# 32 more tokens as gathered expert rows, and a gate matrix added up in DRAM by indirect DMAs

## The chip, the cores and the metric

One core of a Trainium2 chip. The metric is the device time of one execution in microseconds; the time before is the median of three runs.

## What is computed

One layer of a decoder for 512 tokens of 2048 float32 features: two token mixers, a merge, a PEER channel mixer, a gated per-layer input and a last norm. The change lies in the PEER mixer. Per token it scores 8 heads against two tables of 128 keys, takes the 16 best of each half, then the 16 best of their 256 sums; each of these 8 x 16 = 128 choices is one of 16384 experts, with a softmax gate g:

```
z = jnp.einsum('thkd,td->thk', u_tab[eb], hb)
a = jax.nn.gelu(z, approximate=False) * gb
return jnp.einsum('thk,thkd->td', a, v_tab[eb])
```

`eb` are a token's 128 expert numbers, `gb` its gates, `u_tab` and `v_tab` tables of 16384 rows of 2048 floats (128 MB each).

## The kernel before, in words

The tokens are in two groups, and each group has its own way through the PEER mixer.

**Group A, the gathered rows** (128 tokens, one to a partition). For each of its 128 choices s an indirect DMA on POOL (`gather`, L777) fetches 128 rows of 2048 floats, one per token, into one of two buffers `row`. In the u loop VectorE multiplies the row with the token's h and sums it up (`dot_u`, L783; the instruction is L785); in the v loop it adds the row, times its coefficient, to `outA` (`axpy_v`, L1078; L1083). Each of these steps sends the gather for the choice two further on, into the buffer that it has just freed.

**Group B, the dense path** (the other 384 tokens). All 16384 experts are computed: the u loop has 128 steps, each with a block of 128 experts: 16 x 3 = 48 matmuls of 384 columns (`mm3`, L146 to L149; three products of parts, hi and lo, for float32 accuracy). ScalarE takes GELU and stores the result in DRAM (`finish`, z_s). The v loop multiplies z by the gate matrix G (`act_mul`), splits the product into two parts (`act_split`) and multiplies it with the v table: again 128 steps of 48 matmuls, whose sums VectorE adds up (`add_up`, L1091).

**The weights** come through `Ahead`: SP loads a block two steps ahead, ScalarE (L111) and VectorE (L112) split it into hi and lo one step ahead, in four buffers each. Without these splits TensorE has nothing to multiply.

**The gate matrix** has a place for every expert and every token of group B, nearly all zeros. `gate_tokens` (L821) builds it in the u loop: for four tokens at a time ScalarE and VectorE make one-hot matrices (L832, L833, L838), TensorE multiplies them (L843), ScalarE and VectorE bring the result into `stage` (L848, L849), and ACT's queue stores 32 tokens at a time in DRAM (G_s). The v loop loads G by `act_load`.

**Order.** In both loops the order on every engine is the order of the program's text (`tc.manual_schedule`, L871). A list `work` spreads the top-k steps of group B's three blocks of 128 tokens and the building of G over the steps of the u loop: 16 steps of top-k alone, twice 36 steps with the top-k of the next block and G of the last one, then 22 steps with G alone. `dots` spreads the dot products evenly, about 1.07 a step.

Of the kernel before, what the change touches and what calls it, by code (L numbers as in the profile page):

```python
# [20 lines left out]
T = 512  # L21
D = 2048
KT = 16
NA = 128
NB = T - NA
NJ = 8
# [20 lines left out]
def kernel(ctx: ExitStack, tc: tile.TileContext, a, dbg=None):  # L47
# [14 lines left out]
    # ---------------------------------------------------------------- helpers  # L62
# [14 lines left out]
    class Ring:  # L77
        """Buffers taken in turn."""
# [42 lines left out]
    class Ahead:  # L121
        """Streams of a list of blocks: loaded two steps ahead, split one step ahead."""
# [28 lines left out]
    def split(hi, lo, src, gain=None):  # L151
        """hi + lo = src * gain, both float32r."""
# [29 lines left out]
    def rstd_cols(ss, n, name):  # L182
        """[128 tokens, blocks] of 1/sqrt(ss/n + eps)."""
# [13 lines left out]
    def sums_over_features(sq):  # L197
        """[128 tokens, 4] PSUM sums over the partitions of sq [128, T]."""
# [6 lines left out]
    def rows_of(rc, out=None):  # L205
        """[128, tokens], in out or else in PSUM: every partition holds the row of rc."""
# [11 lines left out]
    class SumSq:  # L218
        """Sum of squares of [128, T] chunks over features."""
# [18 lines left out]
    # ---------------------------------------------------------------- constants  # L238
    masks = const.tile([128, 384], F32R, name="masks")
    cst = const.tile([128, 386], F32, name="cst")  # L240
    negmask, ident, iota = cst[:, :128], cst[:, 128:256], cst[:, 256:384]
    freq, sgn = cst[:, 384:385], cst[:, 385:386]
    tril = const.tile([128, 128], U32, name="tril")
# [16 lines left out]
    # ---------------------------------------------------------------- DRAM scratch  # L260
# [7 lines left out]
    z_s = dram.tile([128 // NJ, 128, NJ, NB], F32, name="z_s")  # L268
# [31 lines left out]
    # ---------------------------------------------------------------- HGRN2  # L300
# [147 lines left out]
    # ---------------------------------------------------------------- gates (kept before the sigmoid)  # L448
    def gate_proj(src, dst):
        ps = cols_proj(src, xh, xl)  # L450
# [4 lines left out]
    # ---------------------------------------------------------------- MLA  # L455
# [17 lines left out]
    # rotary tables: angle = position * frequency, reduced to [-pi, pi]  # L473
# [49 lines left out]
    for hp in range(4):  # L523
# [21 lines left out]
        # a head's rotary part: its 64 rows of high parts, and in the other 64 rows their low parts  # L545
# [58 lines left out]
    # ---------------------------------------------------------------- merge  # L604
# [33 lines left out]
    opool.release()  # L638

    # ---------------------------------------------------------------- residual, second norm  # L640
# [20 lines left out]
    hBl = hpool.tile([128, 16, NB], F32R, name="hBl")  # L661
    hrow = hpool.tile([128, D], F32, name="hrow")
# [38 lines left out]
    def topk(b, i1o, i2o, gate):  # L701
        """Steps (cost, function) that fill i1o, i2o, gate: [128 tokens, 8 heads * 16] float32."""
# [57 lines left out]
    # ---- group A: expert rows gathered for the first 128 tokens  # L760
    def prep_A():
# [3 lines left out]
        def experts():  # L765
            V.scalar_tensor_tensor(i1, i1, 128.0, i2, op0=OP.mult, op1=OP.add)
            V.tensor_copy(eA, i1)
            gather(a["peer_u"], 0)
            gather(a["peer_u"], 1)
# [5 lines left out]
    in_flight = {}  # L775

    def gather(tab, s):  # L777
        row = rows()
        G.indirect_dma_start(out=row, out_offset=None, in_=tab,  # L779
                             in_offset=bass.IndirectOffsetOnAxis(ap=eA[:, s:s + 1], axis=0))  # L780
        in_flight[s] = row

    def dot_u(s):  # L783
        row = in_flight.pop(s)
        V.scalar_tensor_tensor(row, row, 1.0, hrow, op0=OP.mult, op1=OP.mult,  # L785
                               accum_out=zA[:, s:s + 1])
        if s + 2 < 128:
            gather(a["peer_u"], s + 2)
        else:
            gather(a["peer_v"], s + 2 - 128)  # L790

    # ---- group B: the gate matrix [i1, i2, token]
    slots = {}
    after_pe, after_pe_next, hold = [], [], [0]

    def prep_B(b):
        i1 = upool.tile([128, 128], F32, name="i1", bufs=2)
        i2 = upool.tile([128, 128], F32, name="i2", bufs=2)
        gt = upool.tile([128, 128], F32, name="gt", bufs=1)

        def turn():
            slots[b] = upool.tile([128, 4, 128], F32, name="slots", bufs=1)

            def pe():
                ps = mx()
                for n, t in enumerate((i1, i2, gt)):
                    TE.transpose(ps[:, n * 128:n * 128 + 128], t, ident)

                def act():
                    S.activation(flat(slots[b][:, :2]), ps[:, :256], AF.Copy)  # L810
                    split(slots[b][:, 2].bitcast(F32R), slots[b][:, 3], ps[:, 256:384])
                return act

            after_pe.append(lambda: after_pe_next.append(pe))
            hold[0] = 2

        return topk(b + 1, i1, i2, gt) + [(0, turn)]

    stage = [None]

    def gate_tokens(t0):  # L821
        """Gate matrices of tokens t0 .. t0+3 of group B."""
        if t0 % TC == 0:
            stage[0] = upool.tile([128, 128, TC], F32, name="stage", bufs=1)
        st = stage[0]
        hot = []
        for i in range(4):
            b, t = divmod(t0 + i, 128)
            l = upool.tile([128, 128], F32R, name="ohl", bufs=8)
            r = upool.tile([128, 2, 128], F32R, name="ohr", bufs=8)  # L830
            i1T, i2T = (slots[b][:, n, t:t + 1] for n in range(2))
            S.activation(l, iota, AF.Abs, scale=-1.0, bias=i1T)  # L832
            V.scalar_tensor_tensor(r, iota[:, None, :].to_broadcast([128, 2, 128]), i2T,  # L833
                                   slots[b][:, 2:4, t:t + 1].to_broadcast([128, 2, 128]),
                                   op0=OP.is_equal, op1=OP.mult)
            hot.append((l, r))
        for l, _ in hot:
            S.activation(l, l.bitcast(F32), AF.Relu, scale=-1.0, bias=ones[:, :1])  # L838
# [537 lines left out]
```

## Time and profile before

| | us |
|---|---|
| median of three runs (4041.59 to 4042.62) | 4041.68 |
| span of the profiled execution | 4040.0 |
| u loop, end of its first step to its end | 1651.7 to 2771.2 |
| v loop | 2771.2 to 3838 |
| first and last one-hot matmul | 1853.4 to 2679.3 |

The profiled execution's own time outside the profile is not listed apart from its span; the median of the runs is 1.7 us above the span. Times in the rows below count from the start of the span. A busy share is an average over stages; what an engine waits for in one stage is read in the table of stretches and in the timelines. PE is TensorE, PEld its weight load, DVE VectorE, ACT ScalarE, POOL GpSimd, SP the engine whose queue loads the weights.

### The profile page before, as it was taken

The numbers are of one execution on the slowest core, as the hardware profiler recorded it, in microseconds if no ns is written. First come the engines' busy times: TensorE is split into PE (matmuls) and PEld (weight loads), VectorE is DVE, ScalarE is ACT, GpSimd is POOL, SyncE is SP. The second block draws the span as 40 slices with busy tenths as digits, with TensorE's granted clock in tenths as the row PEclk, the third lists the DMA queues.
The fourth block names the chain that finished last, engine by engine and source line by source line (L and its number), as shares of the span: only waits on it lengthen the run. The fifth ranks groups of instructions, "written<-read, shape, count | busy, mean of one in ns | idle before, by whom it ended". The sixth has DMA issues, their size and how long they took to land. (4 is left out here: it accounts for less than half of the span.)

```text
span 4040.0 us, 54629 instructions
## 1 busy us (share of the span) xinstructions
PE 4005.3 (99%) x21191; PEld 3667.2 (91%) x21191; DVE 2621.1 (65%) x3992; ACT 1597.2 (40%) x2582; POOL 347.6 (9%) x262
## 2 busy tenths in 40 slices
PE   9999999999999999999999999999999999999998
PEld 7878777778888889999999999999999999999976
DVE  5352554443343343699998998977777888877744
ACT  5342433332332242325566555753333333333443
POOL 0000000000000000021221211111111111111000
PEclk9999999999999999999999999999999999999999
DMA  5222222334444442478787788789888888888432
GB/s 210 97 74 94 72 96 84 102 105 141 151 141 133 141 140 99 166 286 304 283 303 283 287 302 298 293 332 356 317 297 315 312 311 312 299 313 310 169 117 97
DMA packets 264515, 862.68 MB, mean 214 GB/s; under 512 B 24128, under 2 KB 94272, under 8 KB 229568
## 3 DMA queue, kind: packets, MB, share of 16 engines
q1 hardware_dynamic: 202064, 531.57, 38.5%
q0 software_dynamic: 36864, 268.45, 17.8%
q10 hardware_dynamic: 25328, 59.17, 3.8%
q8 instruction: 168, 2.75, 0.3%
q14 instruction: 91, 0.75, 0.1%
HBM read 780.44 MB, written 78.64 MB: 213 GB/s over the span
## 5 line engine op out<-in xcount | busy, mean ns | idle before, releaser
L111 ACT ACTIVATE hi<-raw 128x1024 fp32r<-128x1024 f32 x806 | 851.4, 1059 | 1606.9 <-PE acc L148 1371.9
L112 DVE TENSOR_TENSOR lo<-raw,hi 128x1024 fp32r<-128x1024 f32 x806 | 975.0, 1221 | 782.6 <-ACT hi L111 779.5
L147 PE MATMUL acc<-hBh,hi 128*128 128x384 f32 x2304 | 775.0, 336 | 0.0
L148 PE MATMUL acc<-hBl,hi 128*128 128x384 f32 x2304 | 774.5, 336 | 0.0
L149 PE MATMUL acc<-hBh,lo 128*128 128x384 f32 x2304 | 774.4, 336 | 0.0
L148 PEld LDWEIGHTS acc<-hBl,hi 128*128 128x128 f32 x2304 | 433.1, 188 | 3.0 <-DVE hBl L155 0.2
L147 PEld LDWEIGHTS acc<-hBh,hi 128*128 128x128 f32 x2304 | 433.1, 188 | 2.7
L149 PEld LDWEIGHTS acc<-hBh,lo 128*128 128x128 f32 x2304 | 433.1, 188 | 0.0
L779 POOL DMA_INDIRECT row<-in_peer_u_dram,eA x128 | 198.9, 1554 | 2551.1 <-DMA raw<-in_uT_dram 1703.2
L149 PE MATMUL acc<-xh,lo 128*128 128x512 f32 x912 | 363.9, 399 | 0.0
L147 PE MATMUL acc<-xh,hi 128*128 128x512 f32 x912 | 363.4, 398 | 0.0
L148 PE MATMUL acc<-xl,hi 128*128 128x512 f32 x912 | 362.6, 398 | 0.0
L147 PE MATMUL acc<-ahx,hi 128*128 128x384 f32 x1024 | 344.7, 337 | 0.0
L148 PE MATMUL acc<-alx,hi 128*128 128x384 f32 x1024 | 344.1, 336 | 0.0
L149 PE MATMUL acc<-ahx,lo 128*128 128x384 f32 x1024 | 344.1, 336 | 0.0
L147 PE MATMUL acc<-ah,hi 128*128 128x384 f32 x1024 | 344.1, 336 | 0.0
L148 PE MATMUL acc<-al,hi 128*128 128x384 f32 x1024 | 344.1, 336 | 0.0
L149 PE MATMUL acc<-ah,lo 128*128 128x384 f32 x1024 | 344.1, 336 | 0.0
L1083 DVE SCALAR_TENSOR_TENSOR outA<-row,coef,outA 128x2048 f32<-128x2048 f32 x127 | 298.0, 2346 | 16.6 <-DMA row<-in_peer_v_dram,eA 16.3
L785 DVE SCALAR_TENSOR_TENSOR row<-row,hrow 128x2048 f32<-128x2048 f32 x128 | 292.0, 2283 | 20.5 <-DMA row<-in_peer_u_dram,eA 20.4
L779 POOL DMA_INDIRECT row<-in_peer_v_dram,eA x128 | 147.5, 1152 | 860.3 <-DVE outA L1083 799.6
L149 PEld LDWEIGHTS acc<-xh,lo 128*128 128x128 f32 x912 | 171.4, 188 | 43.0 <-issue 2.4
(379 smaller groups left out, 6270.5 us busy)
## 6 DMA issues: line engine op xcount, KB each, us to landing
raw<-in_uT_dram SPq DMA_DIRECT2D x256, 512.0 KB, 6.9
raw<-in_vB_dram SPq DMA_DIRECT2D x256, 512.0 KB, 5.7
z_s<-t ACTq DMA_DIRECT2D x128, 192.0 KB, 4.9
G_s<-stage ACTq DMA_DIRECT2D x12, 2048.0 KB, 14.4
zt<-z_s SPq DMA_DIRECT2D x32, 768.0 KB, 7.4
gt<-G_s SPq DMA_DIRECT2D x32, 768.0 KB, 12.1
raw<-in_w_ga_dram SPq DMA_DIRECT2D x32, 512.0 KB, 3.5
raw<-in_w_gb_dram SPq DMA_DIRECT2D x32, 512.0 KB, 3.5
```

The lines of the kernel that those rows point to most:

```text
L111: S.activation(hi, raw, AF.Copy)
L112: V.tensor_tensor(lo, raw, hi.bitcast(F32), op=OP.subtract)
L147: TE.matmul(out, lhsT=lh, rhs=rh, start=start, stop=False)
L148: TE.matmul(out, lhsT=lh, rhs=rl, start=False, stop=False)
L149: TE.matmul(out, lhsT=ll, rhs=rh, start=False, stop=stop)
L779: G.indirect_dma_start(out=row, out_offset=None, in_=tab, in_offset=bass.IndirectOffsetOnAxis(ap=eA[:, s:s + 1], axis=0))
L785: V.scalar_tensor_tensor(row, row, 1.0, hrow, op0=OP.mult, op1=OP.mult, accum_out=zA[:, s:s + 1])
L1083: V.scalar_tensor_tensor(outA, row, coef[:, s:s + 1], outA, op0=OP.mult, op1=OP.add)
```

## The change

NX = 32 of the 384 tokens of group B move to the gathered rows; the dense path keeps ND = 352. The 32 tokens are the last of group B. They use all 128 partitions: each token has RX = 4 partitions, each with 32 of its 128 choices (`eX`, `gateX`, `zX`, `hrowX`, `outX`), so there are 32 more gathers for u and 32 more for v. `gather`, `dot_u` and `axpy_v` take their choices from one list, `order`; per step of either loop there are 1.33 dots or additions. At the end the four partial sums of a token are added up (`finish_x2`).

The one-hot matrices go. `clear` fills G_s with zeros, four expert blocks with each of the 32 gate projections that precede the PEER mixer. In the u loop `places` computes where in G_s each gate belongs, and `scatter` adds 128 gates (one choice of 128 tokens; 96 tokens in the last block) into G_s with an indirect DMA that accumulates: 3 x 128 scatters, in heads of 16. The scatters of one head do not wait for one another; those of the next head wait for all 16 of the head before, as two heads can choose the same expert. Blocks come in the order 2, 0, 1. POOL's order is no longer that of the text: the compiler's scheduler places its DMAs.

```diff
+NX = 32
+RX = 128 // NX
+ND = NB - NX
-    G_s = dram.tile([NB // TC, 128, 128 * TC], F32, name="G_s")
+    G_s = dram.tile([128, 128, ND], F32, name="G_s")
...
+    def clear(j0):
+        nc.scalar.dma_start(G_s.rearrange("j i t -> i j t")[:, j0:j0 + 4], zeros[:, None, :].to_broadcast([128, 4, ND]))
+
     def gate_proj(src, dst):
+        clear(4 * (32 - len(gates_todo) - 1))
...
+    order = [(a["peer_u"], 0, s) for s in range(128)] + [(a["peer_u"], 1, s) for s in range(NX)]
+    order += [(a["peer_v"], 1, s) for s in range(NX)] + [(a["peer_v"], 0, s) for s in range(128)]
+
+    def gather():
+        if order:
+            tab, x, s = order.pop(0)
+            row = rows()
+            e = eX if x else eA
+            G.indirect_dma_start(out=row, out_offset=None, in_=tab,
+                                 in_offset=bass.IndirectOffsetOnAxis(ap=e[:, s:s + 1], axis=0))
+            in_flight.append((row, x, s))
+
+    def dot_u():
+        row, x, s = in_flight.pop(0)
+        z = zX if x else zA
+        V.scalar_tensor_tensor(row, row, 1.0, hrowX if x else hrow, op0=OP.mult, op1=OP.mult,
+                               accum_out=z[:, s:s + 1])
+        gather()
...
+        def places():
+            off_b[b] = upool.tile([128, 128], U32, name="off", bufs=2)
+            V.scalar_tensor_tensor(i2, i2, 128.0, i1, op0=OP.mult, op1=OP.add)
+            V.tensor_scalar(i2, i2, float(ND), tcol[:, b:b + 1], op0=OP.mult, op1=OP.add)
+            V.tensor_copy(off_b[b], i2)
...
+    def scatter(b, s):
+        n = min(128, ND - 128 * b)
+        ins = G.indirect_dma_start(out=G_flat, in_=gate_b[b][:n, s:s + 1], in_offset=None,
+                                   out_offset=bass.IndirectOffsetOnAxis(ap=off_b[b][:n, s:s + 1], axis=0),
+                                   compute_op=OP.add).ins
+        if s % 16 == 0:
+            before_head[b], this_head[b] = this_head.get(b, []), []
+        for other in this_head[b]:
+            tc.declare_no_dep(ins, other, reason="a head's experts differ")
+        for other in before_head[b]:
+            tc.add_manual_dep(ins, other.name, SYNC, reason="experts of two heads can be the same")
+        this_head[b].append(ins)
+
+    def gate_tokens(b, s0):
+        for s in range(s0, s0 + 4):
+            scatter(b, s)
...
-    ordered = tc.manual_schedule()
+    ordered = tc.manual_schedule(engines={E.PE, E.DVE, E.Activation, E.SP})
...
-            work = phase(B0, prep_B(0))
-            for b in (1, 2):
-                prep = prep_B(b)
-                work += phase(MIX, merge(prep[:-1], quads[b - 1]) + prep[-1:])
-            work += phase(NW - NF - B0 - 2 * MIX, quads[2])
+            work = phase(B0, prep_B(2))
+            for b, b1 in ((2, 0), (0, 1)):
+                prep = prep_B(b1)
+                work += phase(MIX, merge(prep, quads[b]))
+            work += phase(NW - NF - B0 - 2 * MIX, quads[1])
...
-            while dots and 129 - len(dots) <= 128 * n / (NU - 1 - NF) + 1e-9:
-                dot_u(dots.pop(0))
-        z = acc()[:, :NB]
+            while dots and NDOT + 1 - dots <= NDOT * n / (NU - 1 - NF) + 1e-9:
+                dots -= 1
+                dot_u()
+        z = acc()[:, :ND]
         for k in range(KT):
-            mm3(z, *cur.part(k, KT), hBh[:, k], hBl[:, k], k == 0, k == KT - 1)
+            mm3(z, *cur.part(k, KT), *hBd[k], k == 0, k == KT - 1)
```

On POOL, in the u loop of the kernel before, gathers follow each other; `DVE` in brackets is the wait for the dot that frees the row buffer, and DMASW0 to DMASW7 are the eight semaphores that POOL's DMAs use in turn:

```order
L779 DMA row_9653<-in_peer_u_dram,eA 128x2048 [waits DMASW0_49,DVE_49]
L779 DMA row_9654<-in_peer_u_dram,eA 128x2048 [waits DMASW1_49,DVE_49]
L779 DMA row_9653<-in_peer_u_dram,eA 128x2048 [waits DMASW2_49,DVE_49]
L779 DMA row_9654<-in_peer_u_dram,eA 128x2048 [waits DMASW3_49,DVE_49]
L779 DMA row_9653<-in_peer_u_dram,eA 128x2048 [waits DMASW4_49,DVE_49]
```

On POOL after the change, among the scatters of the last token block (`gt` holds its gates, `off` their places):

```order
L843 DMA G_s<-gt,off 5767168x1 [waits DMASW1_49]
L843 DMA G_s<-gt,off 5767168x1 [waits DMASW2_49]
L800 DMA row_9695<-in_peer_u_dram,eA 128x2048 [waits DMASW3_49,DVE_49]
L843 DMA G_s<-gt,off 5767168x1 [waits DMASW4_49]
L843 DMA G_s<-gt,off 5767168x1 [waits DMASW5_49]
L843 DMA G_s<-gt,off 5767168x1 [waits DMASW6_49]
L843 DMA G_s<-gt,off 5767168x1 [waits DMASW7_49]
L843 DMA G_s<-gt,off 5767168x1 [waits DMASW5_49,DMASW4_49,DMASW6_49,DMASW2_49,DMASW7_49,DMASW1_49,DMASW0_49]
L800 DMA row_9694<-in_peer_u_dram,eA 128x2048 [waits DVE_49]
L800 DMA row_9695<-in_peer_u_dram,eA 128x2048 [waits DVE_49]
```

Scatters now stand between the gathers, and a DMA of POOL waits for the one eight places before it. The scatter with seven semaphores is the first of a head; the gathers behind it on POOL stand behind its wait. Between the first and the last scatter POOL has 384 scatters and 125 gathers.

On VectorE in the last steps of top-k, before (`lo` is the split of the weights, `ohr` the one-hot matrices, `zA` the dot):

```order
L833 SCALAR_TENSOR_TENSOR ohr<-cst,slots 128x256 x4
L785 SCALAR_TENSOR_TENSOR row_9654,zA<-row_9654,hrow 128x2048
L112 TENSOR_TENSOR lo_80<-raw_72,hi_76 128x1024
L112 TENSOR_TENSOR lo_81<-raw_73,hi_77 128x1024
L849 TENSOR_TENSOR stage<-stage,wide 128x128x4
L785 SCALAR_TENSOR_TENSOR row_9653,zA<-row_9653,hrow 128x2048
```

and after, a little behind the top-k of the last block:

```order
L807 SCALAR_TENSOR_TENSOR row_9695,zA<-row_9695,hrow 128x2048
L115 TENSOR_TENSOR lo_80<-raw_72,hi_76 128x1024
L115 TENSOR_TENSOR lo_81<-raw_73,hi_77 128x1024
L807 SCALAR_TENSOR_TENSOR row_9694,zA<-row_9694,hrow 128x2048
L807 SCALAR_TENSOR_TENSOR row_9695,zA<-row_9695,hrow 128x2048
L115 TENSOR_TENSOR lo_82<-raw_74,hi_78 128x1024
L115 TENSOR_TENSOR lo_83<-raw_75,hi_79 128x1024
```

The one-hot work is gone, every third step has two dots, and the splits of the next weights stand behind them.

## Rows read from the trace of the kernel before

**Rows 1.** The page, part 1: span, and busy time of each engine

```profile
span 4040.0 us, 54629 instructions
PE 4005.3 (99%) x21191; PEld 3667.2 (91%) x21191; DVE 2621.1 (65%) x3992; ACT 1597.2 (40%) x2582; POOL 347.6 (9%) x262
```

**Rows 2.** Busy time by stretch: stretch, its length, engines, granted clock, DMA share, GB/s

```profile
1704.90:1850.00 145.10, 145.10 (x840) 145.06 (x839) 136.65 (x312) 50.08 (x69) 32.58 (x20) 1.00 0.83 302
1850.00:2680.00 830.00, 823.18 (x4831) 817.85 (x4830) 749.60 (x1321) 510.09 (x1142) 154.60 (x98) 1.00 0.80 294
2680.00:2771.20 91.20, 91.20 (x528) 91.20 (x527) 60.23 (x62) 29.90 (x41) 15.82 (x12) 1.00 0.96 355
2771.20:3838.00 1066.80, 1066.80 (x6161) 1066.53 (x6160) 843.17 (x922) 350.67 (x406) 143.40 (x126) 1.00 0.84 299
```

**Rows 3.** TensorE's timeline: matmuls 1 and 57 of 384 columns, 1 and 72 of 256

```profile
3199.77 0.34 PE L149 MATMUL acc<-ah,lo 128*128 128x384 f32 x1
...
3209.47 0.34 PE L148 MATMUL acc<-al,hi 128*128 128x384 f32 x1
...
4008.01 0.28 PE L147 MATMUL acc<-x2h,hi 128*128 128x256 f32 x1
...
4016.42 0.27 PE L149 MATMUL acc<-x2h,lo 128*128 128x256 f32 x1
```

**Rows 4.** Instruction groups by line: busy us, mean ns, idle time before them

```profile
L112 DVE TENSOR_TENSOR lo<-raw,hi 128x1024 fp32r<-128x1024 f32 x806 | 975.0, 1221 | 782.6 <-ACT hi L111 779.5 <-PE wide L843 1.7 <-DMA t<-oa 0.2
...
L1083 DVE SCALAR_TENSOR_TENSOR outA<-row,coef,outA 128x2048 f32<-128x2048 f32 x127 | 298.0, 2346 | 16.6 <-DMA row<-in_peer_v_dram,eA 16.3
L785 DVE SCALAR_TENSOR_TENSOR row<-row,hrow 128x2048 f32<-128x2048 f32 x128 | 292.0, 2283 | 20.5 <-DMA row<-in_peer_u_dram,eA 20.4
L779 POOL DMA_INDIRECT row<-in_peer_u_dram,eA x128 | 198.9, 1554 | 2551.1 <-DMA raw<-in_uT_dram 1703.2 <-DVE row L785 844.2 <-DVE lo L112 3.1
...
L833 DVE SCALAR_TENSOR_TENSOR ohr<-cst,slots 128x256 fp32r<-128x256 f32 x384 | 157.6, 477 | 0.1
L779 POOL DMA_INDIRECT row<-in_peer_v_dram,eA x128 | 147.5, 1152 | 860.3 <-DVE outA L1083 799.6 <-DMA row<-in_peer_v_dram,eA 27.5 <-DVE outA L1081 15.0
```

**Rows 5.** POOL's timeline in the u loop: start, length, idle time before

```profile
1829.35 0.94 POOL L779 DMA_INDIRECT row<-in_peer_u_dram,eA  x1 [6.90 <-DVE row L785]
...
1837.87 1.68 POOL L779 DMA_INDIRECT row<-in_peer_u_dram,eA  x1 [4.23 <-DVE row L785]
...
1960.69 2.75 POOL L779 DMA_INDIRECT row<-in_peer_u_dram,eA  x1 [9.42 <-DVE row L785]
1963.74 1.98 POOL L779 DMA_INDIRECT row<-in_peer_u_dram,eA  x1 [0.31 <-issue]
```

**Rows 6.** VectorE's timeline beside two of these gathers

```profile
1837.51 2.36 DVE L112 TENSOR_TENSOR lo<-raw,hi 128x1024 fp32r<-128x1024 f32 x2
...
1960.34 2.28 DVE L785 SCALAR_TENSOR_TENSOR row<-row,hrow 128x2048 f32<-128x2048 f32 x1
```

**Rows 7.** DMA issues: count, KB each, median us from issue to landing

```profile
z_s<-t ACTq DMA_DIRECT2D x128, 192.0 KB, 4.9
...
oa<-kT SPq DMA_DIRECT2D x8, 256.0 KB, 2.0
...
row<-in_peer_u_dram,eA POOLq DMA_INDIRECT x128, 9.0
row<-in_peer_v_dram,eA POOLq DMA_INDIRECT x128, 6.8
```

**Rows 8.** Waits: total us, times, longest

```profile
POOL row L779 <- DVE row L785: 851.5, 125, 17.3
```

**Rows 9.** VectorE's timeline in the v loop, where two row additions follow each other

```profile
3015.46 4.73 DVE L1083 SCALAR_TENSOR_TENSOR outA<-row,coef,outA 128x2048 f32<-128x2048 f32 x2
...
3025.79 2.35 DVE L1083 SCALAR_TENSOR_TENSOR outA<-row,coef,outA 128x2048 f32<-128x2048 f32 x1 [1.46 <-DMA row<-in_peer_v_dram,eA]
```

More of the change, by code (lines that the diff above doesn't have):

```diff
@@ L661 @@
     hBl = hpool.tile([128, 16, NB], F32R, name="hBl")
+    hBd = [(hBh[:, k, :ND], hBl[:, k, :ND]) for k in range(16)]
     hrow = hpool.tile([128, D], F32, name="hrow")
@@ L773, in prep_A @@
         return topk(0, i1, i2, gateA) + [(1, experts)]
[L775 to L794, printed above, removed]
+    in_flight = []
+    order = [(a["peer_u"], 0, s) for s in range(128)] + [(a["peer_u"], 1, s) for s in range(NX)]
[13 more added lines that the diff above has]
+                               accum_out=z[:, s:s + 1])
+        gather()
+    off_b, gate_b = {}, {}
+    before_head, this_head = {}, {}
     def prep_B(b):
@@ L817, in prep_B @@
[L817 to L838, printed above, removed]
-        def pe():
-            ps = wide()
-            for i, (l, r) in enumerate(hot):
-                TE.matmul(ps[:, i * 256:i * 256 + 256], lhsT=l, rhs=flat(r), start=True, stop=True)
-            def act():
-                o = t0 % TC
-                hi, lo = (ps.rearrange("p (t s j) -> p s j t", t=4, s=2)[:, n] for n in range(2))
-                S.activation(st[:, :, o:o + 4], hi, AF.Copy)
-                V.tensor_tensor(st[:, :, o:o + 4], st[:, :, o:o + 4], lo, op=OP.add)
-                if o == TC - 4:
-                    nc.scalar.dma_start(G_s[t0 // TC], flat(st))
-            return act
-        after_pe.append(pe)
-        if t0 % TC == TC - 4:
-            hold[0] = 2
@@ new lines, in prep_B, with experts_X @@
+        gt = gate_b[b] = upool.tile([128, 128], F32, name="gt", bufs=2)
+        def experts_X():
+            e, x = t2()[:, :128], slice(128 - NX, 128)
+            V.scalar_tensor_tensor(e[x], i1[x], 128.0, i2[x], op0=OP.mult, op1=OP.add)
+            for r in range(RX):
+                V.tensor_copy(eX[r * NX:(r + 1) * NX], e[x, r * NX:(r + 1) * NX])
+                S.activation(gateX[r * NX:(r + 1) * NX], gt[x, r * NX:(r + 1) * NX], AF.Copy)
+        def places():
[3 more added lines that the diff above has]
+            V.tensor_copy(off_b[b], i2)
@@ L861, in merge @@
         return [lists[n][i] for _, n, i in sorted(order)]
[L863 removed]
+    quads = [[(2, lambda b=b, s=s: gate_tokens(b, s)) for s in range(0, 128, 4)] for b in range(3)]
     def phase(steps, work):
@@ L918, in rows_of_h, with rows_of_hX @@
         S.activation(hrow[:, c * 512:(c + 1) * 512], ps, AF.Copy)
+    def rows_of_hX(c):
+        o = slice(c * 4, c * 4 + 4)
+        t = t2()
+        t4 = t.rearrange("p (k r t) -> p k r t", k=4, r=RX)
+        V.tensor_tensor(t4, hBh[:, o, None, ND:].bitcast(F32).to_broadcast([128, 4, RX, NX]),
+                        hBl[:, o, None, ND:].bitcast(F32).to_broadcast([128, 4, RX, NX]), op=OP.add)
+        ps = mx()
+        for k in range(4):
+            s = slice(k * 128, k * 128 + 128)
+            TE.transpose(ps[:, s], t[:, s], ident)
+        S.activation(hrowX[:, c * 512:(c + 1) * 512], ps, AF.Copy)
     pending = None
@@ L979 @@
     start_up = {2: by_group[3], 3: rest[:4], 4: rest[4:7], 5: rest[7:9], 6: rest[9:]}
-    dots = list(range(128))
+    NDOT = 128 + NX
+    dots = NDOT
     def finish(z, j):
-        zg = t2()[:, :NB]
+        zg = t2()[:, :ND]
         S.activation(zg, z, AF.Gelu)
@@ L1018 @@
             n = j + 1 - NF
-            hold[0] = max(0, hold[0] - 1)
-            while work and spent < n and not hold[0] and len(after_pe) < 2:
+            while work and spent < n:
                 c, f = work.pop(0)
@@ L1073, with axpy_v @@
         r.tiles = [r.tiles[(r.at + i) % NJ] for i in range(NJ)]
-        r.tiles = r.tiles + [vwC.tile([128, NB], F32R, name=f"{name}x{i}") for i in range(NJ)]
+        r.tiles = r.tiles + [vwC.tile([128, ND], F32R, name=f"{name}x{i}") for i in range(NJ)]
         r.at = NJ
     assert len(aT) == NJ
-    def axpy_v(s):
-        row = in_flight.pop(s)
+    def axpy_v():
+        row, x, s = in_flight.pop(0)
+        o, c = (outX, coefX) if x else (outA, coef)
         if s == 0:
-            V.tensor_scalar(outA, row, coef[:, 0:1], None, op0=OP.mult)
+            V.tensor_scalar(o, row, c[:, 0:1], None, op0=OP.mult)
         else:
-            V.scalar_tensor_tensor(outA, row, coef[:, s:s + 1], outA, op0=OP.mult, op1=OP.add)
-        if s + 2 < 128:
-            gather(a["peer_v"], s + 2)
+            V.scalar_tensor_tensor(o, row, c[:, s:s + 1], o, op0=OP.mult, op1=OP.add)
+        gather()
+    S.activation(coefX, zX, AF.Gelu)
+    V.tensor_tensor(coefX, coefX, gateX, op=OP.mult)
     S.activation(coef, zA, AF.Gelu)
@@ L1099 @@
     late = []
-    axpys = list(range(128))
+    axpys = NDOT
     NV = (NGRP - 1) * 8
```

87 lines of the change are left out of this document (43 added, 44 removed).

## The prediction

> **What bounds the kernel now.** I read the engine shares first: TensorE is busy 99% of a span of 4040.0 us, VectorE 65%, POOL (GpSimd) 9% [rows 1]. Shares average over stages, so the table of stretches comes next [rows 2]. The change lies in two loops: the u loop (128 steps of 48 matmuls, its last step ending at 2771.2 us) and the v loop (128 steps, 2771.2 to 3838). In both, TensorE is busy without a gap or nearly so, and the clock granted is 1.00, the upper level of 2.4 GHz. A shorter matmul is therefore worth its time, as long as nothing else becomes late. The same table shows what is close behind: VectorE at 749.6 of 830 us in the main part of the u loop, and DMA engines busy 0.80 to 0.96 of the time.
>
> POOL looks free: in 830 us it is busy 154.6 us [rows 2]. What it does the rest of the time is in the waits: 851.5 us for VectorE's dot product to give back one of two row buffers [rows 8]. A gather is thus sent as soon as a buffer is free, and POOL has nothing else to do. That is what the change ends.
>
> **TensorE.** A matmul of 384 columns starts every 9.70/56 = 0.1732 us, one of 256 columns every 8.41/71 = 0.1185 us, each with a new weight block [rows 3]. Interpolated, 352 columns take 0.1595 us. A step of 48 goes from 8.32 to 7.66 us; over 256 steps that is 168 us. The 384 one-hot matmuls go too; they and their waits are the rest of the u loop's 8.83 us per step in 1850 to 2680 (94 steps). Were TensorE still the bound there, that stretch would take 94 x 7.66 = 720 us instead of 830. The transposes for the 32 new tokens are 32 of about 0.1 us, +4 us with their waits.
>
> **VectorE.** Gone: 384 building instructions of 477 ns [rows 4] and the 96 stage adds. New: 32 dots of 2283 ns and 32 row additions of 2346 ns [rows 4], 1.33 a step instead of 1.07. In 1704.9 to 1850 VectorE is busy 136.7 of 145.1 us [rows 2] with top-k and no one-hot work; 16 x 0.27 more dots add 9 us there and use up the stretch, so I give these steps no gain (bounds: 0 and -15 us).
>
> **POOL in the 94 steps of 1850 to 2680.** The order of instructions has 384 scatters and 125 gathers between the first and the last scatter, against 98 gathers in that stretch today [rows 2]. Each scatter is an indirect DMA with 128 indices (96 in one token block), like a gather. What a scatter costs POOL no row shows; the nearest rows are the gathers. Alone, a gather is 0.94 us; when VectorE is in a dot as it begins, 2.75 us; next to the split of the weights, 1.68 us [rows 5]. The dot began at 1960.34 and ran 2.28 us [rows 6]; 2.75 is the rest of that dot plus 0.9. So POOL waits for VectorE's current instruction and then takes its own 0.94 us. To each comes the 0.30 us gap before the next one [rows 5]. The bounds are 0.94 + 0.30 = 1.24 and 2.75 + 0.30 = 3.05 us. I take the mean of the u gathers, 1.55 + 0.30 = 1.85 us [rows 4], because scatters meet the same VectorE work of the same loop: 509 x 1.85 = 943 us (bounds 631 and 1552).
>
> The Trainium skill ("SBUF — State Buffer", section "Who interferes with whom") says that a VectorE instruction with two SBUF inputs blocks a GpSimd instruction that reads SBUF until it has ended; the gathers agree (2.75 us), and since a scatter reads its offsets there, the rule speaks against scatters at 1.24 us.
>
> To this come waits that POOL makes in order. The first scatter of each head waits until all 16 of the head before have landed; everything behind it on POOL, gathers too, stands still. That is 23 waits. A landing of a small write in this stretch is at least that of the z stores, 4.9 us, and at most that of a gather, 9.0 us; in stages with idle DMA engines 2.0 us is seen [rows 7]. I take 4.9: 113 us (bounds 46 and 207).
>
> For the fixed part of a DMA from POOL the Trainium skill ("DMA: Bandwidth & Descriptors", section "Anatomy of one DMA") states about 2.0 us. By that figure the waits would be an estimated 46 us and my sum 67 us lower.
>
> Together the stretch needs 943 + 113 = 1056 us of POOL, more than the 720 us of TensorE. This is on the path, not beside it: the gathers stand between the scatters, a dot waits for its gather, VectorE is in order, and behind the dot on VectorE stand the splits without which TensorE has no weights. So the stretch takes 1056 instead of 830 us, **+226 us**.
>
> **The last 11 steps of the u loop** (91.2 us now [rows 2]) have gathers but no scatters; at the v loop's pace below they gain at most 3 us: 0.
>
> **The v loop.** Where two row additions follow each other today, the first starts at 3015.46, and its buffer is next used at 3025.79, 1.46 us late because of the DMA [rows 9]: 10.33 us. With 1.33 additions a step every third step has two. Three steps then cost this 10.33 us plus two steps of VectorE work at 2.28 (two splits) + 2.27 + 4 x 0.43 = 6.27 us: 22.9 us, just TensorE's 3 x 7.66 = 23.0. Nothing is left for slower transfers, and these come: bytes per step rise from 2.56 to 2.81 MB while the step shrinks, 299 GB/s [rows 2] to 367. Gathers land in 6.8 us here and 9.0 us in the u loop [rows 7]; I take 1.3 us of that difference of 2.2 as the added landing, because the load grows but loses its 512-byte packets. 24.2 / 3 = 8.06 us a step: 120 x 8.06 + 8 x 7.66 = 1028 us against 1066.8, **-38 us** (bounds -85 with no added landing, 0 with all 2.2 us).
>
> **At nothing:** 32 clearing DMAs of 0.72 MB on ACT's queue, beside the gate projections, where TensorE is the bound; laid open they would be 23 MB, some 70 us at the 355 GB/s of [rows 2]. ACT loses one-hot work and stays off the path. VectorE's new adds in the last 8 steps of the v loop stand where no row additions do.
>
> **Sum:** 4040.0 + 226 - 38 + 4 = 4232 us of span, +1.7 us between this span and the median of the runs shown (4041.68): 4234 us. A measurement of this kernel can tell about 0.2%, 8 us.
>
> **Rivals.**
> *POOL keeps up (0.21), the other sign.* If scatters mostly find VectorE idle or need fewer cycles than a gather, POOL needs 631 + 113 = 744 us; then the gathers' chain sets the pace, 94 x 8.06 = 758 us: 4040 - 72 - 38 + 4 + 2 = 3936 us. The stretch may grow by the 38 - 4 us won elsewhere before the kernel is slower, to 864 us; the rival thus decides below a mean of (864 - 113) / 509 = 1.48 us per indirect DMA, gap included. For it: the v gathers average 1.15 + 0.30 = 1.45 us [rows 4]. Against it: in the u loop the split and dots take more of VectorE's time.
> *The accumulating DMAs are slow to land (0.13).* Each POOL DMA waits for the eighth before it (the eight semaphores in the order of POOL). At 9 us a landing that is 509 x 9/8 = 573 us, hidden. It decides from about 16 us; at 25 us the stretch is 1590 us and the time 4767 us. No row has a 4-byte read-and-add in DRAM, so I cannot exclude it.
> *The matmul is no shorter (0.02),* because a weight load of 188 ns is longer than 0.1595 us. The 256-column matmuls start every 0.1185 us with the same loads [rows 3], so this is nearly out; it would cost the v loop's 38 us: 4272.
>
> **How the numbers follow.** The forecast, POOL sets the pace of the u loop, has 0.64, with a range of its own of 4040 to 4400. The range of 8 in 10 leaves out the slow landings and the tail of the fast rival: 3935 to 4460. Faster by over 0.2%: the first rival, 0.21. Within 0.2%: the lowest edge of the forecast, 0.03. Slower: the rest, 0.76.
>
> **What would show it.** Right: in the u loop POOL is busy most of the time, "DVE row waits for DMA" grows from 20 us to hundreds, TensorE has gaps at the weight splits, 352-column matmuls start every 0.16 us in the v loop, and the last u steps run at about 8 us. Wrong: scatters of about 1 us on POOL beside a full TensorE in the u loop (first rival), or scatter landings of tens of us with POOL waiting on its own DMAs (second).

## The result, and the profile after

The changed kernel takes 4390.76 us (median of four runs, 4389.81 to 4396.26), against 4041.64 us (median of four runs of the kernel before): a ratio of 1.0865, 95% interval 1.085 to 1.088. The forecast of 4234 us had the sign and its range of 3935 to 4460 holds the time, but 157 us of the loss are not in its sum. The profiled execution took 4389.81 us, its span 4388.0.

The page, part 1 of the kernel after, answers to [rows 1]: TensorE is busy 89% of its span instead of 99%, and POOL three times as long as before.

```profile
span 4388.0 us, 52887 instructions
PE 3920.1 (89%) x20830; PEld 3567.3 (81%) x20830; DVE 2542.9 (58%) x3656; ACT 1303.1 (30%) x1721; POOL 1085.0 (25%) x711
```

Busy time by stretch of the kernel after, with the columns of [rows 2]. The four are: the top-k steps without scatters, the steps with scatters, the last steps of the u loop, the v loop.

```profile
1715.00:1867.00 152.00, 135.73 (x800) 133.70 (x799) 136.84 (x314) 43.39 (x56) 34.01 (x22) 0.94 0.80 288
1867.00:3083.00 1216.00, 817.78 (x4542) 804.17 (x4541) 610.56 (x913) 241.47 (x294) 848.66 (x510) 0.83 0.70 207
3083.00:3171.00 88.00, 82.61 (x499) 80.87 (x498) 62.03 (x64) 27.35 (x38) 20.72 (x15) 0.98 0.95 357
3171.00:4186.00 1015.00, 1006.37 (x6161) 1003.58 (x6161) 899.82 (x983) 334.21 (x406) 180.00 (x158) 1.00 0.92 344
```

The second row is the loss: in 1216 us TensorE works 818, VectorE 611, POOL 849. No engine is busy all the time. The granted clock there is 0.83 on average, between the two levels of 1.2 and 2.4 GHz, while TensorE stands idle a third of the stretch. In the v loop the clock is 1.00 and TensorE again full.

The GELU of each step (L984 before, L1004 after; 128 of them) dates the steps. Between the first GELU and that of step 23 the kernel loses 28.0 us (222.1 against 194.1), in the 94 steps to step 117 it loses 368.5 (1211.5 against 843.0), then 4.1 to the end of the u loop, and from there to the end (the v loop and the last stage) it gains 51.3 (1217.6 against 1268.9). With 1.3 us won ahead of the u loop the sum is the whole difference of the spans, 348.0 us.

Waits of the kernel after in the scatter stretch (total us, times, longest), the answer to [rows 8]:

```profile
DVE row L807 <- DMA row<-in_peer_u_dram,eA: 469.2, 67, 29.3
...
PE acc L152 <- DVE lo L115: 398.2, 47, 24.6
POOL row L800 <- DVE row L807: 172.4, 39, 7.0
DVE row L807 <- DMA row<-in_peer_u_dram,eX: 134.1, 14, 15.2
POOL G_s L843 <- issue: 127.5, 359, 5.5
...
POOL G_s L843 <- DMA G_s<-gt,off: 37.7, 22, 6.4
...
POOL row L800 <- issue: 21.9, 72, 0.3
POOL row L800 <- DMA G_s<-gt,off: 3.8, 6, 2.3
```

Read from the top this is the chain of the prediction: VectorE waits 603 us for rows, and TensorE waits 398 us for the splits that stand behind the dots on VectorE. VectorE's account closes with its rows alone: busy 611 and 603 of these waits are 1214 of 1216 us, so neither TensorE nor its lower clock holds VectorE up here. The POOL lines give its 1216 us: busy 849, gaps between DMAs 149 ("issue"), waits for scatters to land 41.5, and 172 us in which POOL itself waits for a dot to free a row. In the same stretch POOL waits for VectorE and VectorE for POOL.

How both happen shows in the timelines of POOL and VectorE around 2501 us:

```profile
2499.48 1.54 POOL L843 DMA_INDIRECT G_s<-gt,off  x1 [0.30 <-issue]
2501.33 1.00 POOL L800 DMA_INDIRECT row<-in_peer_u_dram,eA  x1 [0.30 <-issue]
2505.34 2.02 POOL L843 DMA_INDIRECT G_s<-gt,off  x1 [3.02 <-DMA G_s<-gt,off]
...
2535.13 1.54 POOL L843 DMA_INDIRECT G_s<-gt,off  x1 [0.30 <-issue]
2536.98 1.00 POOL L800 DMA_INDIRECT row<-in_peer_u_dram,eA  x1 [0.30 <-issue]
```

```profile
2508.49 2.29 DVE L807 SCALAR_TENSOR_TENSOR row<-row,hrow 128x2048 f32<-128x2048 f32 x1 [2.56 <-DMA row<-in_peer_u_dram,eA]
...
2542.38 2.29 DVE L807 SCALAR_TENSOR_TENSOR row<-row,hrow 128x2048 f32<-128x2048 f32 x1 [29.31 <-DMA row<-in_peer_u_dram,eA]
```

Between the two gathers the compiler put 16 scatters. By 2510.8, at the end of the upper dot, both buffers were free; the next gather went out at 2537.0, and VectorE stood still for 29.3 us. Over all 125 dots of the stretch the gather into the freed buffer starts 8.7 us after the dot's end on average (0.3 us before the change); a gather's start to its dot is 8.3 us and a dot 2.3. Two buffers share this ring of 19.3 us, so 9.66 us a dot, and 125 of them make 1207 us: the stretch. This sum says where the time lies; what it depends on, the experiments below test.

### The profile page after: what moved, and what is told of

It reads as the page before. It is cut to its first block, busy times and chain, and to the rows that moved or that the text cites. A ratio compares the mean times of both kernels' runs of the same rounds, so it can differ in the third digit from the quotient of the medians.

```text
span 4388.0 us, 52887 instructions
## 1 busy us (share of the span) xinstructions
PE 3920.1 (89%) x20830; PEld 3567.3 (81%) x20830; DVE 2542.9 (58%) x3656; ACT 1303.1 (30%) x1721; POOL 1085.0 (25%) x711
## 5 line engine op out<-in xcount | busy, mean ns | idle before, releaser
L114 ACT ACTIVATE hi<-raw 128x1024 fp32r<-128x1024 f32 x806 | 844.9, 1056 | 1986.9 <-PE acc L151 1482.9
L152 PE MATMUL acc<-hBh,lo 128*128 128x352 f32 (+1 forms) x2304 | 793.4, 344 | 417.8 <-DVE lo L115 417.7
L150 PE MATMUL acc<-hBh,hi 128*128 128x352 f32 (+1 forms) x2304 | 783.2, 340 | 0.0
L151 PE MATMUL acc<-hBl,hi 128*128 128x352 f32 (+1 forms) x2304 | 779.8, 338 | 0.0
L843 POOL DMA_INDIRECT G_s<-gt,off x384 | 688.1, 1792 | 170.3 <-issue 127.5
L800 POOL DMA_INDIRECT row<-in_peer_u_dram,eA x128 | 173.0, 1352 | 1552.1 <-DVE eA L783 1244.3
L150 PE MATMUL acc<-ah,hi 128*128 128x352 f32 x1024 | 335.5, 328 | 1.4 <-ACT hi L114 1.4
L150 PE MATMUL acc<-ahx,hi 128*128 128x352 f32 x1024 | 335.3, 327 | 0.5 <-DVE x L1107 0.5
L152 PE MATMUL acc<-ah,lo 128*128 128x352 f32 x1024 | 334.4, 327 | 0.7 <-DVE lo L115 0.7
L151 PE MATMUL acc<-al,hi 128*128 128x352 f32 x1024 | 331.7, 324 | 3.5 <-DVE al L158 3.5
L151 PE MATMUL acc<-alx,hi 128*128 128x352 f32 x1024 | 331.2, 323 | 4.0 <-DVE alx L158 3.9
L152 PE MATMUL acc<-ahx,lo 128*128 128x352 f32 x1024 | 333.9, 326 | 0.6 <-DVE lo L115 0.5
```

The costliest lines, as they stand in the source:

```text
L114: S.activation(hi, raw, AF.Copy)
L150: TE.matmul(out, lhsT=lh, rhs=rh, start=start, stop=False)
L151: TE.matmul(out, lhsT=lh, rhs=rl, start=False, stop=False)
L152: TE.matmul(out, lhsT=ll, rhs=rh, start=False, stop=stop)
L800: G.indirect_dma_start(out=row, out_offset=None, in_=tab, in_offset=bass.IndirectOffsetOnAxis(ap=e[:, s:s + 1], axis=0))
L843: ins = G.indirect_dma_start(out=G_flat, in_=gate_b[b][:n, s:s + 1], in_offset=None, out_offset=bass.IndirectOffsetOnAxis(ap=off_b[b][:n, ...
```

## The experiments

Two theories. **A, POOL's stream:** the sum of what POOL issues (scatters, gathers, gaps) paces the u loop. **B, the place in the stream:** a gather comes late because it stands behind a run of scatters, whatever POOL's total. A rival to both is that the extra gathers, not the scatters, slow the loop.

**No scatters.**

```diff
     def gate_tokens(b, s0):
-        for s in range(s0, s0 + 4):
-            scatter(b, s)
+        return
```

> Leaves out all 384 accumulating DMAs, so the gate matrix stays zero; the 32 gathered tokens, the 352 columns, the clearing and the loads of the gate matrix stay. Theory A (POOL's scatters pace the u loop): the 1216 us of the scatter stretch fall to the pace of TensorE or of the gathers' chain, 7.7 to 8.1 us a step; the u loop ends near 2700 us and the kernel takes 3910 to 3950 us. Rival (the 32 extra gathers or the load on the DMA engines slow the u loop, and scatters only stand beside it): over 4150 us. VectorE's wait for rows falls from 600 us to below 60 by theory A and stays above 300 by the rival.

Measured: 3949.97 us. The 94 steps take 767.7 us, 8.17 each, a little over the expected pace, and POOL waits for VectorE again:

```profile
POOL row L800 <- DVE row L807: 575.6, 125, 7.5
...
DVE row L807 <- DMA row<-in_peer_u_dram,eA: 126.0, 50, 5.8
...
DVE row L807 <- DMA row<-in_peer_u_dram,eX: 33.9, 13, 4.5
```

VectorE's waits for rows fall from 603 to 160 us in the steps, between the two expected values (below 60, above 300): some waits are there without any scatter, and what a third buffer does about such waits, a run further below shows. So the scatters cost 440 us, and the rest of the change gains 92 (3950 against 4042) while nothing builds the gate matrix; the rival is out as a cause of the loss.

**Half of them.**

```diff
-        for s in range(s0, s0 + 4):
+        for s in range(s0, s0 + 4, 2):
```

> Leaves out every second scatter (192 remain). If POOL's throughput alone counts: 192 x (1.79 + 0.30) + 125 x (1.35 + 0.30) = 607 us of POOL in the stretch, less than TensorE's 720, so the time is within 30 us of the kernel without scatters. If the place of the gathers behind runs of scatters counts (each gather comes late, whatever POOL's total): about half of the loss stays, some 200 us above the kernel without scatters.

Measured: 4169.28 us, 219 above the run without scatters: half the loss. Its scatter stretch, and waits in it:

```profile
1867.00:2770.00 903.00, 704.84 (x4046) 694.35 (x4045) 549.87 (x859) 214.13 (x259) 497.61 (x302) 0.89 0.76 245
```

```profile
DVE row L807 <- DMA row<-in_peer_u_dram,eA: 318.7, 59, 18.2
POOL row L800 <- DVE row L807: 288.8, 62, 7.2
```

POOL is busy 498 us, with 86 us of gaps and 27 of waits between heads: 611 of 903. It is not full, it waits 289 us for dots, and yet VectorE waits 342 us for rows (319 for `eA`, 24 for `eX`). Theory A alone is out; B holds here.

**A third row buffer in the u loop.**

```diff
+    row2 = xpool2.tile([128, D], F32, name="row2")
+    free.append(row2)
...
-            row = rows()
+            row = free.pop(0)
```

> A third row buffer in the u loop, nothing else. POOL is busy 849 of the 1216 us, 150 us are gaps of 0.30 us, 172 us it waits for a dot to free a row while elsewhere VectorE waits 603 us for rows. If the two engines lose time to each other through two buffers: 120 to 200 us faster than 4390. If POOL's own stream is the bound and its waits are only where VectorE is itself late: less than 50 us.

Measured: 4358.51 us, 32 less, as the second expectation has it. A buffer more helps little while the gathers stand where they stood: the gather now starts 16.5 us after the dot that freed its row instead of 8.7, and POOL still waits 112 us for dots in the scatter steps. So two buffers are not the main cause.

**An even order on POOL.**

```diff
     def gate_tokens(b, s0):
         for s in range(s0, s0 + 4):
-            scatter(b, s)
+            sc_todo.append((b, s))
...
+            chain(G.indirect_dma_start(out=row, out_offset=None, in_=tab,
+                                       in_offset=bass.IndirectOffsetOnAxis(ap=e[:, s:s + 1], axis=0)).ins, True)
+            if tab is a["peer_u"]:
+                scatters(4 if len(sc_todo) > 8 else 3)
```

`chain` keeps POOL in that order without waits.

> The same DMAs, but POOL's order fixed: after each gather three scatters (four where a backlog of over eight stands), then the next gather, instead of the compiler's order with runs of up to 18 scatters between gathers. If the order costs (gathers late behind runs of scatters): POOL becomes busy without pause and the stretch takes 384 x 2.09 + 125 x 1.65 = 1009 us plus some 40 us of waits for a head, so 150 to 200 us faster than 4390. If POOL's throughput is the bound already: within 50 us of 4390.

Measured: 4323.66 us, 67 less: between the two expectations. (The longest run of scatters in the compiler's order is 16, not 18.) What holds the rest, the next run shows.

**Even order and third buffer.** Both edits together.

> The changed kernel with both reliefs: three scatters after each gather, and a third row buffer. POOL's own stream in the scatter stretch is 384 x (1.89 + 0.30) + 127 x (1.45 + 0.30) + 40 us of waits between heads = 1103 us, against some 1150 us with the even order alone (POOL still waited for dots). If POOL's throughput is the floor that is left: 4250 to 4295 us, not lower. If the chain through the buffers was the whole cost: below 4200 us.

Measured: 4322.84 us, no better than the even order alone. The window of its scatter steps (columns as in [rows 2]):

```profile
1872.00:2984.00 1112.00, 828.71 (x4506) 812.41 (x4504) 602.33 (x890) 240.15 (x291) 861.56 (x484) 0.86 0.75 222
```

and the waits of POOL and of VectorE in it:

```profile
DVE row L822 <- DMA row<-in_peer_u_dram,eA: 360.2, 74, 11.3
...
POOL G_s L859 <- issue: 116.0, 328, 5.0
POOL G_s L859 <- DMA G_s<-gt,off: 95.4, 27, 8.3
...
POOL row L813 <- issue: 32.9, 108, 0.3
```

POOL's waits for dots are gone from these 1112 us. Busy 861.6 + gaps 148.9 + waits between heads 95.4 = 1106: POOL is full. The expectation of a gain was wrong because the even order alone is already full, not at 1150 us as reckoned: in the same window it has 860 busy, 157 of gaps, 62 between heads and 30 waiting for dots, 1108 of 1112. The even order won 100 us in the 94 steps (1112 against 1211.5); 31 of them it gives back in the last steps (117.6 instead of 86.5 us), where the scatters left over lie. What is left of the loss in the 94 steps with the even order, 269 us (1112 against 843), goes with a full POOL, theory A, and the run after the next shows that the time then follows POOL's work. The two parts do not simply add up: with half the scatters POOL was not full, and yet half the loss was there. Whether POOL's waits between heads cost time in the even order was not tried.

**Write instead of add.**

```diff
-                                   out_offset=bass.IndirectOffsetOnAxis(ap=off_b[b][:n, s:s + 1], axis=0),
-                                   compute_op=OP.add).ins
+                                   out_offset=bass.IndirectOffsetOnAxis(ap=off_b[b][:n, s:s + 1], axis=0)).ins
```

> The 384 scatters write instead of adding (the compute operation is left out, so where two heads of a token choose the same expert one gate is lost). Their number, places, order and waits stay. If the addition makes a scatter dear for POOL (1.55 us median beside 1.00 us for an undisturbed gather): about 0.5 us less each, 100 to 200 us faster than 4390. If POOL's price is that of the 128 indices and the read and add only happens on the DMA's way: scatters stay at 1.55 us median and the time within 30 us of 4390; only the landing of 4.6 us may fall.

Measured: 4232.14 us, 159 less. The scatter's group, of the changed kernel and of this run:

```profile
L843 POOL DMA_INDIRECT G_s<-gt,off x384 | 688.1, 1792 | 170.3 <-issue 127.5 <-DMA G_s<-gt,off 37.7 <-ACT hi L114 4.5
```

```profile
L843 POOL DMA_INDIRECT G_s<-gt,off x384 | 491.3, 1279 | 170.6 <-issue 133.8 <-DMA G_s<-gt,off 32.0 <-ACT hi L114 4.5
```

The mean falls by 0.51 us, the median from 1.55 to 0.96, the price of a gather. The time from the start of the issue to landing stays (4.6 and 4.5 us median). So the addition is paid by POOL as it issues the DMA, not on the DMA's way. It grows with the elements: the first 128 scatters, of the block of 96 tokens, are shorter than the 256 of 128 elements (ns, least, median and most; the first two lines with the addition, the others without):

```profile
L843 POOL DMA_INDIRECT G_s<-gt,off x128: 1416/1437/3418, 1867.7 to 2183.9; - x128
L843 POOL DMA_INDIRECT G_s<-gt,off x256: 1543/1560/3586, 2290.9 to 3080.4; - x128
```

```profile
L843 POOL DMA_INDIRECT G_s<-gt,off x128: 904/913/3032, 1867.5 to 2135.4; - x128
L843 POOL DMA_INDIRECT G_s<-gt,off x256: 953/961/3038, 2241.3 to 2917.0; - x128
```

The addition takes 0.51 us for 96 elements and 0.59 for 128.

**Even order, third buffer and write.** All three.

> The same with scatters that write instead of adding (a gate is lost where two heads of a token choose the same expert). An undisturbed scatter falls from 1.55 to 0.96 us. If POOL's throughput is the floor: 384 x 0.59 = 227 us less than with the addition, limited by the pace of 8.3 us a step seen without scatters: 4020 to 4090 us. If something else holds the loop: less than 120 us of gain.

Measured: 4139.18 us, 184 less than with the addition. The scatter's mean fell from 1.90 to 1.40 us: 384 x 0.505 = 194. Where POOL is full, a microsecond less on POOL is nearly a microsecond less in all. The expected 227 took the fall of the undisturbed scatter for all of them. The time is above the expected range, and POOL is still full here: busy 675.5, 155 of gaps and 72 of waits between heads are 903 of 926 us in its stretch:

```profile
1867.00:2793.00 926.00, 778.63 (x4492) 768.48 (x4490) 603.71 (x905) 237.64 (x288) 675.50 (x481) 0.91 0.78 266
```

**No waits between heads.**

```diff
+    G_h = [G_s] + [dram.tile([128, 128, ND], F32, name=f"G_h{i}") for i in range(1, 8)]
...
-    ins = G.indirect_dma_start(out=G_flat, in_=gate_b[b][:n, s:s + 1], in_offset=None,
+    ins = G.indirect_dma_start(out=G_flats[s // 16], in_=gate_b[b][:n, s:s + 1], in_offset=None,
...
-            before_head[b], this_head[b] = this_head.get(b, []), []
+            before_head[b], this_head[b] = [], []
```

> Each of the eight heads scatters into a matrix of its own, and no head waits for the one before it; the v loop reads the first head's matrix only, so seven eighths of the gates are left out of the result. The prediction took 23 waits of 4.9 us, 113 us. By the trace after the change POOL idles 37.7 us in 22 such waits. By the prediction's term: some 110 us faster; by the trace: 20 to 50 us faster, part of it taken back because POOL then waits for dots instead.

Measured: 4395.25 us, no gain, and neither expectation holds. The waits went, and POOL waits longer for dots instead (397 against 345 us over the u loop). In the compiler's order these waits are not on the path.

**The two parts of the change, each alone.** First 352 columns with the one-hot gate matrix:

```diff
-    ordered = tc.manual_schedule(engines={E.PE, E.DVE, E.Activation, E.SP})
+    ordered = tc.manual_schedule()
...
-        for s in range(s0, s0 + 4):
-            scatter(b, s)
...
+            V.scalar_tensor_tensor(r, iota[:, None, :].to_broadcast([128, 2, 128]), i2T,
+                                   slots[b][:, 2:4, t:t + 1].to_broadcast([128, 2, 128]),
+                                   op0=OP.is_equal, op1=OP.mult)
```

> Only the first part of the change: 32 more gathered tokens and 352 columns, with the gate matrix built by one-hot matmuls as before. If the scatters make the whole loss: the v loop keeps its gain of 51 us, and the u loop ends 0 to 60 us earlier than before (VectorE is busy 750 + 58 us of 830 in the one-hot stretch, so little is left there): 3930 to 3995 us. If the extra gathers cost the u loop time as well: 4020 us and more.

Measured: 4095.74 us, 53 slower than before: a miss. The u loop loses 83 us, from the v loop to the end 27 are won. Its one-hot stretch:

```profile
1869.00:2764.00 895.00, 833.11 (x4870) 804.08 (x4869) 796.69 (x1353) 492.98 (x1091) 204.23 (x126) 0.95 0.83 305
```

VectorE is busy 797 us and waits 82 for rows: 879 of 895. With one-hot work and 1.33 dots a step the path runs through VectorE, at 9.5 us a step; whether the 82 us of waits had to be, the run after the next shows.

Then the scatters with 384 columns and no extra gathers:

```diff
-NX = 32
-RX = 128 // NX
+NX = 0
...
-            e = eX if x else eA
+            e = eA
```

> Only the second part of the change: the gate matrix by accumulating indirect DMAs, with 384 columns and 128 gathered tokens as before. If the scatters alone make the loss: about the loss of the scatters in the changed kernel (4390 - 3950 = 440 us, less some for fewer gathers and more TensorE time to cover them) on a kernel of some 4020 us: 4350 to 4460 us. If they need the extra gathers to hurt: below 4250 us.

Measured: 4479.64 us, 437 slower than before, a little over the range; from the v loop to the end it is as before within 0.2 us. The 437 us are not to be set beside the 440 of the run without scatters, since there nothing took the scatters' place. Scatters instead of one-hot work cost 437 us with 384 columns, and 295 with 352 columns and the extra gathers (4390.76 against 4095.74). Why the first is more is open; POOL waits 288 us for dots there, against 172 in the changed kernel, in another order by the compiler:

```profile
POOL row L799 <- DVE row L806: 287.6, 49, 9.4
```

**Versions that might beat both.** The one-hot version with 352 columns and the third buffer of the u loop, the edits of both runs above:

> The 32 extra gathered tokens with the one-hot gate matrix, and a third row buffer in the u loop. In the run without it the one-hot stretch took 895 us with VectorE busy 797 and waiting 82 us for rows. If the two-buffer chain (dot, gather, landing) costs the extra gathers their gain: the 82 us go, 4010 to 4055 us. If VectorE's own work is the limit, or the landings only grow: 4080 us and more.

Measured: 4031.11 us (median of six), a ratio of 0.997 to the kernel before (0.9957 to 0.9982). VectorE's waits for rows in the stretch go from 82 to about 5 us, the stretch from 895 to 833:

```profile
1865.00:2698.00 833.00, 808.14 (x4861) 783.76 (x4860) 795.37 (x1352) 491.38 (x1089) 246.28 (x126) 0.98 0.87 326
```

```profile
DVE row L800 <- DMA row<-in_peer_u_dram,eA: 4.5, 3, 3.1
```

The third buffer, worth little among the scatters, is what the extra gathers need. VectorE's own work, 795 of 833 us, is now the limit there.

Last, the same with scatters for the last 96 dense tokens only, set one by one between the gathers:

```diff
+            if tab is a["peer_u"]:
+                scatters(2 if s % 8 == 7 else 1)
...
-    quads = [[(2, lambda b=b, s=s: gate_tokens(b, s)) for s in range(0, 128, 4)] for b in range(3)]
...
+            work = phase(B0, prep_B(2)) + phase(20, prep_B(0))
+            prep = prep_B(1)
+            work += phase(44, merge(prep[:-1], quads[0]) + prep[-1:])
+            work += phase(NW - NF - B0 - 64, quads[1])
```

> 32 extra gathered tokens, 352 columns, three row buffers in the u loop; the gate matrix of the last 96 dense tokens by accumulating scatters (128 of them, one behind each gather, two behind every eighth), that of the other 256 tokens by one-hot matmuls. POOL then has 128 x 2.1 + 125 x 1.8 = 494 us of work in some 850 us. If scatters are harmless as long as POOL's stream has room and a gather never stands behind a run of them: VectorE saves 96 x 0.477 + 24 x 0.68 = 62 us and TensorE 12, so 3980 to 4030 us, no slower than the 4031 us of the one-hot version with three buffers. If every scatter costs its share whatever the order (the 1.1 us apiece seen when half were left out): 4031 + 141 - 62 = 4110 us or more.

Measured: 3976.2 us (median of four), 0.9839 of the kernel before (0.9823 to 0.9856), a little below the first expectation and the fastest of all that compute the whole result. Its stretch, and the scatter's group:

```profile
1872.00:2640.00 768.00, 750.08 (x4666) 741.96 (x4665) 728.18 (x1181) 417.06 (x861) 474.78 (x249) 0.99 0.94 338
```

```profile
L802 POOL DMA_INDIRECT G_c<-gtS,off x128 | 259.5, 2028 | 83.4 <-issue 46.8 <-DMA G_c<-gtS,off 36.6
```

A scatter holds POOL longer here (2.03 us on average for 96 elements, against 1.68 for those of the changed kernel), with VectorE busy 728 of 768 us beside it, and no cost of it can be seen: POOL is busy 475 of 768 us, VectorE waits 17 us for rows, TensorE is busy 750. A scatter has no fixed share of the time; in these runs it cost time where POOL was full or a gather stood behind a run of them. Which of the three in which its scatters differ from the changed kernel's (a third of the number, their places, the third buffer) would be enough was not tried apart.

## Why the prediction was right, and where its sum was short

- **The mechanism held.** Dots wait for gathers, gathers stand behind scatters, splits behind dots: "DVE row waits for DMA" went from 20 to 633 us. Without scatters the time is 3950, near the 3936 us of the rival in which POOL keeps up, and the 94 steps take 768 us against its 758.
- **"POOL in the 94 steps": the mis-sized term.** Taken 943 + 113 = 1056 us; the steps took 1211.5. The parts: (a) 510 indirect DMAs at 1.85 us; measured (848.7 + 149.4) / 510 = 1.96, so 55 us more. The price of an undisturbed scatter was taken from the gather, 0.94 [rows 5]; it is 1.42 us for 96 elements and 1.54 for 128, since adding costs POOL 0.51 and 0.59 us. That this did not weigh more goes with a VectorE that, itself waiting, blocks POOL less: the u gathers for `eA` fell from 1554 to 1352 ns on average. (b) Waits between heads, 23 of 4.9 us; measured 41.5 us in all, 71 less, and taking them away gave nothing. (c) The missing part: 172 us of POOL waiting for dots. By luck the first two nearly cancel, and the 1056 us are close to POOL's own 849 + 149 + 41.5 = 1040; the whole error of 155 us is 55 - 71 + 172. The step that failed is "the stretch takes 1056": a sum of POOL's own work is a floor, nearly reached only with the even order (1106 and 1108 of 1112 us). In the compiler's order POOL stands at a gather whose row is not free at one time and has a run of scatters before the gather at another; a third buffer alone did not change that (32 us).
- **The rule on shared SBUF access** (the Trainium skill, "SBUF — State Buffer", "Who interferes with whom"), that a VectorE instruction with two SBUF inputs contends with a GpSimd instruction that reads SBUF, agrees with this trace:

```profile
2439.39 2.29 DVE L807 SCALAR_TENSOR_TENSOR row<-row,hrow 128x2048 f32<-128x2048 f32 x1 [9.01 <-DMA row<-in_peer_u_dram,eA]
```

```profile
2439.81 3.29 POOL L843 DMA_INDIRECT G_s<-gt,off  x1 [0.30 <-issue]
```

  The dot ends at 2441.68, 1.87 us after the scatter began; 3.29 - 1.87 leaves 1.42 us. This scatter has 128 elements, and undisturbed it would take 1.54: 0.12 us of its work passed beside the dot. It was so with the gather of [rows 5] too: 2.75 us less the dot's rest of 1.93 leaves 0.82, not the 0.9 of the prediction, and a gather alone takes 0.94.
- **The fixed part of a DMA, about 2.0 us** (the Trainium skill, "DMA: Bandwidth & Descriptors", "Anatomy of one DMA") gave an estimated 46 us of waits between heads; measured are 41.5. The nearness is luck: a scatter lands in 4.6 us median, from 2.7 to 9.6, and part of a landing passes while POOL is still at its own issue and at other DMAs, as in the timeline above, where a gather stands between the last scatter of a head and the wait. The shortest landing of a plain scatter was 2.0 us.
- **VectorE in the top-k steps: 0, bounds 0 and -15.** Wrong in sign: steps 7 to 23 take 9.21 instead of 8.32 us, +14. With a third buffer they take 8.76 (8.70 with the even order too), so about half was the two-buffer ring with 1.33 dots a step. Another 14 us lie in steps 0 to 6; there TensorE waits 12.4 us for VectorE to lay out the rows of the 32 tokens. The sum has +4 us for all transposes of these tokens and their waits, so this term was too small.
- **The v loop: -38 us; measured -51** to the end of the kernel, but not for the reason given. A matmul of 352 columns starts every 12.25/75 = 0.1633 us (forecast 0.1595), as the first and the 76th in TensorE's timeline show:

```profile
3399.72 0.33 PE L150 MATMUL acc<-ahx,hi 128*128 128x352 f32 x1
...
3411.97 0.33 PE L150 MATMUL acc<-ahx,hi 128*128 128x352 f32 x1
```

  A step is 1015/128 = 7.93 instead of 8.06 us. The added landing was 1.2 us (6.8 to 8.0 us for `eA`), near the 1.3 taken; yet TensorE is busy 1006 of the 1015 us, so the shorter matmul sets the pace there and not the chain of additions and gathers from which the 8.06 us came. The one-hot version wins only 27 us here, although its columns are the same: TensorE waits 21 us in its v loop for the split of the product with G (L158), against 7 in the changed kernel's. What makes that split late is open; the one-hot version loads G in pieces of 512 bytes, the changed kernel in pieces of 1408, and that was not tried apart.
- **The last steps** at nothing: steps 117 to 127 take 86.5 instead of 82.4 us, 4 us more. **The clearing** at nothing: right, ahead of the u loop 1.3 us were won. **Slow landings** are out: 4.6 us median, 9.6 at most, where that rival decides from about 16.

## What to carry to other kernels

When work moves to an engine that looks idle, add up its stream, then look at who stands behind whom in it: a sum is a floor, and an order left to the compiler can miss it: here the sum was 1040 us, and the steps took 1211.5. The 384 scatters cost 440 us; 128 of them, one behind each gather (two behind every eighth) with a buffer to spare, cost nothing that can be seen. Price an instruction from its own kind: the addition alone made an undisturbed scatter 1.6 times as dear.

## What the runs showed of the hardware

- Undisturbed, an accumulating indirect DMA of 128 four-byte elements held POOL 1.54 us and one of 96 elements 1.42; the same DMAs as plain writes held it 0.95 and 0.90, and a gather of 128 rows of 8 KB 0.94 to 1.00. Between POOL's DMAs lay 0.30 us. The time from issue to landing did not depend on the addition (4.6 and 4.5 us median).
- VectorE's dot held up an indirect DMA of POOL until the dot's end: a gather took 2.75 us and a scatter 3.29, each 0.12 us less than the dot's rest and its undisturbed time together.
- Taking the waits between heads off POOL gave nothing (4395 against 4391 us): it waited for dots instead, 397 against 345 us over the u loop.
- The granted clock fell to 0.83 where TensorE was idle a third of the stretch, though it had been 1.00 in the same steps before; a matmul of 352 columns lasted 342 to 350 ns on average there, against 323 to 327 in the v loop at 1.00.
